# Output projections as seven half-sized products over pairs of 512-token stretches, in place of plain block products

## The chip, the cores and the metric

The kernel runs on one core of one Trainium2 chip. The metric is the device time of one execution in microseconds (us); less is better. The engines are TensorE (PE, with its weight loads shown apart as PEld), VectorE (DVE), ScalarE (ACT), GpSimd (POOL) and SyncE (SP, whose queue issues the transfers). A line number such as L929 is a line of the kernel before.

## The reference, cut to what matters

A decoder layer over 2048 tokens of width 1024 (16 meta tokens are put in front and dropped at the end). One input projection feeds a sliding-window attention branch and an mLSTM branch. What the change touches is the end of it:

```python
y_a = (att * jax.nn.silu(a_z)) @ w_attn_out
y_m = (hm * jax.nn.silu(m_z)) @ w_mlstm_out          # hm: LayerNorm over heads, times head_norm
merged = jax.nn.sigmoid(g_a) * y_a + jax.nn.sigmoid(g_m) * y_m
out = h + rmsnorm(merged @ w_out, norm_post)
```

Each of the three matrices is 1024 x 1024, so there are three products of 2048 x 1024 by 1024 x 1024. Everything is float32.

## The kernel before, in words

**Precision.** A float32 matrix product is made of three matmuls of the type float32r: each operand is split into a rounded part "hi" and a remainder "lo" (`lo = raw - hi`), and hi x hi, hi x lo and lo x hi are added up in one PSUM bank. The rounding is a copy on ACT (L181, L889), the subtraction is DVE's (L182, L890). The operands of the split are plain float32 tiles, 128 partitions by 512 columns (the constant SB).

**The main part** (to about three quarters of the span) goes over two halves of the tokens. For each it runs a plan of 18 column blocks of the input projection (`token_proj`, L703, and `feat_proj`, L715), and weaves the chains of the attention blocks (`attn_block`) and of the mLSTM blocks (`mlstm_chain`) in between: `slot` advances them after every six matmuls. The branches' results go out to memory as att_d and hm_d, feature by token; the gates' as az, mz, ga, gm (`evict_f`). The last two blocks of the plan are those of the gate gm, when all chains of the half are through. PE's order is the order of the program; the other engines' queues are filled by a scheduler by priorities, in which `tc.high_priority(offset=n)` moves instructions ahead by n places. Each engine works its queue in order. In `mlstm_chain` the normalised block, two transposes of 128 columns, is copied out of PSUM by one ACT copy (L611).

**The output projections** (L882 to L971) go over four strips of 512 tokens. For either branch (ph 0 and 1) a strip loads eight tiles of the branch and eight of its gate, multiplies them on DVE (L915; L917 for the mLSTM branch, where the head norm hn_t is a third factor), splits them (`split_unit`, L889 and L890), loads and splits the weights in two halves of eight tiles (`load_w`), and makes eight feature tiles of 24 matmuls each (L929). A bank is evicted on DVE with the merge gate (L934, or L936 and L937), and the merged tile is split at once (L938). Then the third product with w_out (L951) has the merged tiles as the stationary operand; its banks are squared on ACT for the norm (L956), multiplied by gpost (L959, L967), scaled, added to x (L970) and written out. So a strip has 16 + 8 groups of 24 matmuls, 576, and the weights are loaded and split anew in every strip. All tiles of the main part's pools (`units`, `wp`, `stage` and the PSUM pools) stay in use; only the pool `wk` of the main part is closed before, and `p2` takes its place. The operands of the first strip's first branch are loaded ahead by a priority offset of 150.

Of the kernel before, what the change touches and what calls it, by code (L numbers as in the profile page):

```python
# [9 lines left out]
F32 = mybir.dt.float32  # L10
# [80 lines left out]
def hybrid_layer(ctx: ExitStack, tc: tile.TileContext, x, xT, mx, mxT, gpre, w_all, w2, negs, cw, cb,  # L91
# [11 lines left out]
    units = pool("units", 16)  # L103
    wp = pool("wp", 9)
    stage = pool("stage", 4)
    ps_p = pool("ps_p", 2, PSUM)
    ps_s = pool("ps_s", 2, PSUM)
    ps_t = pool("ps_t", 2, PSUM)
    ps_a = pool("ps_a", 2, PSUM)

    def ctile(name, shape, dt=F32):
        return const.tile(shape, dt, name=name)
# [50 lines left out]
    def load_w(src, off, w, p2=None, each=None, lead=SPLIT_LEAD):  # L163
        his, los = [], []
        first = each is not None
        for k in range(KT):
            if first:
                each(k, 0)
            if p2 is None and seq[0] % 5 >= 3:
# [7 lines left out]
            own = p2 is not None and k < 2  # L177
            hi = p2.tile([128, SB], R, name="whi2", bufs=4) if own else wp.tile([128, SB], R, name="whi")
            lo = p2.tile([128, SB], R, name="wlo2", bufs=4) if own else wp.tile([128, SB], R, name="wlo")
# [25 lines left out]
    with ExitStack() as es1:  # L205
# [354 lines left out]
        def mlstm_chain(h, b, j, v1, tho, qT, kT, GT, mrep):  # L560
# [50 lines left out]
            S.copy(tho, th[:, 0:256])  # L611
# [140 lines left out]
        for c in range(NHALF):  # L752
# [7 lines left out]
            for pi, (kind, arg, cols) in enumerate(PLAN):  # L760
# [3 lines left out]
                if c == 0 and pi == 0:  # L764
# [13 lines left out]
                    wh, wl = load_w(w_all, off, w, None, each)  # L778
# [103 lines left out]
    # ---- output projections  # L882
    p2 = pool("p2", 2)
    gpost_t = p2.tile([128, D], F32, name="gpost", bufs=1)
    nc.sync.dma_start(out=gpost_t, in_=gpost.partition_broadcast(128))

    def split_unit(src):
        un = units.tile([128, 2, SB], R, name="un")
        S.copy(un[:, 0], src)  # L889
        tt(un[:, 1], src, f(un)[:, 0], ALU.subtract)  # L890
        return un

    for s in range(SEQ // SB):
        sl = slice(s * SB, (s + 1) * SB)
        part = [None] * KT
        mg = [None] * KT
        for ph, (src, zn, gn) in enumerate(((att_d, "az", "ga"), (hm_d, "mz", "gm"))):
            us = []
            with (tc.high_priority(offset=150) if s == 0 and ph == 0 else ExitStack()):
                for k in range(KT):  # L900
                    early = s == 0 and ph == 0
                    if early:
                        a = p2.tile([128, SB], F32, name=f"part{k}", bufs=1)
                    else:
                        a = stage.tile([128, SB], F32, name="xs")
                    nc.sync.dma_start(out=a, in_=src[k, :, sl])
                    if early:
                        if k % 2 == 0:
                            zz = p2.tile([128, D], F32, name="y", bufs=4)
                        z = zz[:, k % 2 * SB:(k % 2 + 1) * SB]  # L910
                    else:
                        z = p2.tile([128, SB], F32, name="zl", bufs=3)
                    nc.sync.dma_start(out=z, in_=gate_d[zn][k, :, sl])
                    if ph == 0:
                        tt(a, a, z, ALU.mult)  # L915
                    else:
                        stt(a, a, hn_t[:, k:k + 1], z, ALU.mult, ALU.mult)  # L917
                    us.append(split_unit(a))
            for nb_ in range(2):
                wh, wl = load_w(w2, (2 * ph + nb_) * D * SB, SB, p2)  # L920
                for i in range(4):
                    j = nb_ * 4 + i
                    th = p2.tile([128, SB], F32, name="tl", bufs=3)
                    nc.sync.dma_start(out=th, in_=gate_d[gn][j, :, sl])
                    ps = ps_p.tile([128, SB], F32, name="pj")
                    n = 0
                    for k in range(KT):
                        for a, ww in ((0, wh), (1, wh), (0, wl)):
                            T.matmul(ps, lhsT=ww[k][:, 128 * i:128 * i + 128], rhs=us[k][:, a],  # L929
                                     start=(n == 0), stop=(n == 3 * KT - 1))  # L930
                            n += 1
                    if ph == 0:
                        part[j] = p2.tile([128, SB], F32, name=f"part{j}", bufs=1)
                        stt(part[j], th, 1.0, ps, ALU.add, ALU.mult)  # L934
                    else:
                        stt(th, th, 1.0, ps, ALU.add, ALU.mult)  # L936
                        tt(part[j], part[j], th, ALU.add)  # L937
                        mg[j] = split_unit(part[j])  # L938
        w_o = load_w(w2, 4 * D * SB, SB, p2)
        ys, sss = [], []  # L940
        for i in range(4):
            ys.append(p2.tile([128, D], F32, name="y", bufs=4))
            sss.append(p2.tile([128, 4], F32, name="yss", bufs=4))
        for nb_ in range(2):
            wh, wl = w_o if nb_ == 0 else load_w(w2, 5 * D * SB, SB, p2)
            for i in range(4):
                ps = ps_p.tile([128, SB], F32, name="pj")
                n = 0
                for k in range(KT):
                    for a, ww in ((0, wh), (0, wl), (1, wh)):  # L950
                        T.matmul(ps, lhsT=mg[k][:, a, 128 * i:128 * i + 128], rhs=ww[k],  # L951
                                 start=(n == 0), stop=(n == 3 * KT - 1))
                        n += 1
                y, ss = ys[i], sss[i]
                jk = p2.tile([128, SB], BF, name="jk2", bufs=1)
                S.activation(jk, ps, AF.Square, accum_out=ss[:, nb_:nb_ + 1])  # L956
                cs = slice(nb_ * SB, (nb_ + 1) * SB)
                if nb_ == 0:
                    tt(y[:, cs], ps, gpost_t[:, cs], ALU.mult)  # L959
                    ts(ss[:, 2:3], ss[:, 0:1], 1.0 / D, 16.0 * EPS, ALU.mult, ALU.add)  # L960
                    continue
                r0 = s * SB + i * 128
                xr = p2.tile([128, D], F32, name="xr")
                nc.sync.dma_start(out=xr, in_=x[r0:r0 + 128, :])
                ts(ss[:, 2:3], ss[:, 1:2], 1.0 / D, ss[:, 2:3], ALU.mult, ALU.add)  # L965
                G.tensor_tensor(ss[:, 3:4], ss[:, 2:3], mh_t[:, 0:1], ALU.pow)  # L966
                tt(y[:, cs], ps, gpost_t[:, cs], ALU.mult)  # L967
                for j in range(2):
                    cs = slice(j * SB, (j + 1) * SB)
                    stt(y[:, cs], y[:, cs], ss[:, 3:4], xr[:, cs], ALU.mult, ALU.add)  # L970
                    nc.sync.dma_start(out=out[r0:r0 + 128, cs], in_=y[:, cs])  # L971
# [54 lines left out]
```

## Time and profile before

| | |
|---|---|
| three runs | 2420.58, 2423.35, 2424.9 us; median 2423.35 |
| profiled execution: time and span | 2425.5 us |
| granted TensorE clock, mean over the span | 0.994 |
| PE, DVE, ACT, POOL busy, share of the span | 98%, 61%, 42%, 21% |
| output projections: first matmul of L929 to last of L951 | 1875.2 to 2419.5 us |

A share of busy time is an average over parts with different limits; what ends the waits in the part that is changed says more. Matmuls overlap one another, so the record of one (389 ns) is longer than the distance from one to the next. In a timeline a row stands for one or more equal instructions in a row (x2): the first number is when it starts, the second how long it lasts from its first start to its last end. An engine's records overlap a little (a DVE record begins before the one ahead has ended), so the distance of starts tells what one costs in the queue. A record begins when the instruction is taken up, and what it then waits for inside the engine is counted in.

### The profile page before, as it was taken

To read this page: it belongs to the slowest core of one execution; us is meant where nothing else is said; L and a number is where in the kernel's file an instruction comes from. 1 tells how busy PE (TensorE), PEld (TensorE's weight loads), DVE (VectorE), ACT (ScalarE), POOL (GpSimd) and SP (SyncE) were. 2 spreads that over 40 slices of the span, in tenths; PEclk is the share of its full clock that TensorE was granted. 3 is DMA by queue.
4 is the path that set the end of the run, shared out by engine and by line. 5 is a ranking of instruction groups with operands and counts; after the bars stand their busy time and mean duration, and the time that the engine had idled before them with its cause. 6 is when DMAs were issued, how large, how long until landed. Compare 5 with 4: busy or idle time off the path is not lost.

```text
span 2425.5 us, 35347 instructions
## 1 busy us (share of the span) xinstructions
PE 2380.6 (98%) x11725; PEld 2021.0 (83%) x11725; DVE 1469.0 (61%) x4013; ACT 1022.7 (42%) x2674; POOL 517.7 (21%) x1087
## 2 busy tenths in 40 slices
PE   8999999999999999999999999999999999999998
PEld 7788988988888888888988888898888878877787
DVE  7776377367637733677468457637733666665654
ACT  6554354355435423454345345435423333333432
POOL 5332233223233310332323222223310000000000
PEclk8999999999999999999999999999999999999999
DMA  5113212231311234112212212221226768575752
GB/s 188 46 50 101 91 56 67 70 109 42 99 49 58 87 102 142 49 59 70 89 59 58 77 47 65 73 88 56 71 85 226 242 192 263 176 240 168 241 170 92
DMA packets 176167, 261.42 MB, mean 108 GB/s; under 512 B 18684, under 2 KB 68176, under 8 KB 175984
## 3 DMA queue, kind: packets, MB, share of 16 engines
q1 hardware_dynamic: 175984, 259.17, 34.1%
q8 instruction: 92, 1.51, 0.3%
q14 instruction: 91, 0.75, 0.1%
HBM read 200.35 MB, written 58.76 MB: 107 GB/s over the span
## 4 chain that ended last, share of the span: by engine, by line
PE 84%; DMA 6%; DVE 5%; ACT 2%; POOL 1%; issue 1%; SPq 0%; DVEq 0%; POOLq 0%; ACTq 0%
PE pj L715 35%; PE pj L703 22%; PE pj L929 10%; PE pj L951 3%; PE acc L476 3%; PE s L427 3%; DMA wraw<-in_w 3%; DVE wlo L182 2%; PE acc L543 2%; PE tr L449 1%; DMA xs<-att_d 1%; DMA zl<-mz_d 1%; ACT whi L181 1%; PE tr L400 1%; PE tr L543 1%
## 5 line engine op out<-in xcount | busy, mean ns | idle before, releaser
L715 PE MATMUL pj<-un,whi 128*128 128x512 f32 x2560 | 805.0, 396 | 0.0
L703 PE MATMUL pj<-whi,un 128*128 128x512 f32 (+2 forms) x1952 | 604.9, 371 | 0.0
L715 PEld LDWEIGHTS pj<-un,whi 128*128 128x128 f32 x2560 | 467.6, 189 | 88.6
L715 PE MATMUL pj<-un,wlo 128*128 128x512 f32 x1280 | 502.1, 392 | 0.0
L182 DVE TENSOR_TENSOR wlo<-wraw,whi 128x512 fp32r<-128x512 f32 (+2 forms) x480 | 327.1, 704 | 176.1 <-ACT whi L181 173.3
L703 PEld LDWEIGHTS pj<-whi,un 128*128 128x128 f32 x1952 | 361.4, 188 | 38.2 <-issue 1.3
L181 ACT CAST whi<-wraw 128x512 fp32r<-128x512 f32 (+2 forms) x480 | 285.1, 606 | 235.0 <-DMA wraw<-in_w 133.2
L703 PE MATMUL pj<-wlo,un 128*128 128x512 f32 (+2 forms) x976 | 356.3, 365 | 0.0
L929 PE MATMUL pj<-un,whi 128*128 128x512 f32 x1024 | 315.7, 389 | 4.0 <-DVE part L934 4.0
L715 PEld LDWEIGHTS pj<-un,wlo 128*128 128x128 f32 x1280 | 240.7, 188 | 53.1
L929 PEld LDWEIGHTS pj<-un,whi 128*128 128x128 f32 x1024 | 191.9, 188 | 45.4 <-DVE part L934 4.3
L929 PE MATMUL pj<-un,wlo 128*128 128x512 f32 x512 | 199.2, 389 | 0.0
L703 PEld LDWEIGHTS pj<-wlo,un 128*128 128x128 f32 x976 | 184.1, 189 | 15.0
L459 POOL TENSOR_SCALAR_AFFINE_SELECT pp<-pc 128x512 fp32r<-128x512 f32 x120 | 84.0, 700 | 436.0 <-ACT pc L454 420.3
L951 PE MATMUL pj<-whi,un 128*128 128x512 f32 x512 | 163.4, 398 | 10.2 <-DVE y L967 8.1
L728 ACT ACTIVATE xs<-pj 128x512 f32<-128x512 f32 x128 | 76.5, 598 | 213.9 <-PE pj L715 197.8
L433 ACT ACTIVATE P<-s,mn 128x144 f32<-128x144 f32 x256 | 97.5, 381 | 125.5 <-DVE junk L431 122.0
L966 POOL TENSOR_TENSOR yss<-yss,mhalf 128x1 f32<-128x1 f32 x16 | 8.8, 550 | 618.8 <-DVE yss L965 618.8
L951 PEld LDWEIGHTS pj<-whi,un 128*128 128x128 f32 x512 | 98.3, 192 | 33.4 <-DVE y L967 9.3
L929 PEld LDWEIGHTS pj<-un,wlo 128*128 128x128 f32 x512 | 96.1, 188 | 20.0 <-DVE wlo L182 0.2
L951 PE MATMUL pj<-wlo,un 128*128 128x512 f32 x256 | 101.3, 396 | 0.0
L429 DVE COPY_PREDICATED s<-um,s 128x128 f32<-128x128 int32 x240 | 65.7, 292 | 58.5 <-PE s L427 58.1
(334 smaller groups left out, 3373.7 us busy)
## 6 DMA issues: line engine op xcount, KB each, us to landing
wraw<-in_w_all SPq DMA_DIRECT2D x224, 256.0 KB, 3.4
wraw<-in_w SPq DMA_DIRECT2D x192, 256.0 KB, 3.5
wraw<-in_w_all SPq DMA_DIRECT2D x48, 192.0 KB, 2.5
ga_d<-xs SPq DMA_DIRECT2D x32, 256.0 KB, 2.4
att_d<-ao SPq DMA_DIRECT2D x64, 128.0 KB, 1.8
hm_d<-tho SPq DMA_DIRECT2D x64, 128.0 KB, 1.8
az_d<-xs SPq DMA_DIRECT2D x32, 256.0 KB, 2.4
mz_d<-xs SPq DMA_DIRECT2D x32, 256.0 KB, 2.4
```

The costliest lines, as they stand in the source:

```text
L181: S.copy(hi[:, :w], raw[:, :w])
L182: tt(lo[:, :w], raw[:, :w], f(hi)[:, :w], ALU.subtract)
L427: T.matmul(sp[:, c0:272], lhsT=qs[:, h // 2, h % 2, :], rhs=ks[:, i, c0:272], start=(i == 0), stop=(i == 1))
L433: S.activation(P[:, s], sp[:, 128:272], AF.Exp, bias=mn[:, s:s + 1], scale=-1.0, accum_out=mn[:, 4 + s:5 + s])
L459: G.affine_select(pp[:, i], f(pc)[:, i], pattern=[[0, 4], [-1, 128]], compare_op=ALU.is_gt, fill=0.0, base=0, channel_multiplier=1)
L476: T.matmul(acc, lhsT=l, rhs=r.rearrange("p s q -> p (s q)"), start=(i == 0), stop=(i == len(ops) - 1))
L543: T.matmul(out, lhsT=l[:, a], rhs=r[:, b_], start=(start and n == 0), stop=(stop and n == 2))
L703: T.matmul(ps[:, :w], lhsT=us[k][:, a, o:o + 128], rhs=ww[k][:, :w], start=(n == 0), stop=(n == 3 * KT - 1))
L715: T.matmul(ps, lhsT=ww[k][:, 128 * i:128 * i + 128], rhs=us[k][:, a], start=(n == 0), stop=(n == 3 * KT - 1))
L728: S.activation(th, ps, AF.Tanh, scale=0.5)
L929: T.matmul(ps, lhsT=ww[k][:, 128 * i:128 * i + 128], rhs=us[k][:, a], start=(n == 0), stop=(n == 3 * KT - 1))
L951: T.matmul(ps, lhsT=mg[k][:, a, 128 * i:128 * i + 128], rhs=ww[k], start=(n == 0), stop=(n == 3 * KT - 1))
```

## The change

The four strips become two pairs of 512-token stretches, and each of the three products is made for a pair as a 2 x 2 block product in Winograd's form of Strassen's method. The matrix is cut in two along the contraction (512 of 1024) and in two along the output features, the tokens in two along the stretches. Names: w00, w01, w10, w11 are quarters of the weights (first digit the contraction half, second the feature half), b00 to b11 quarters of the data (contraction half, stretch). Seven products of 48 matmuls, P1 to P7, are made of these and of sums and differences of them:

- weights: s3 = w00 - w01, s2 = w11 - s3, s1 = s2 + w00, s4 = w10 - s2, on POOL; s3, s1 and s4 are written over w01, w00 and w10, s2 has two tiles of its own
- data: t1 = b01 - b00, t2 = b11 - t1, t3 = b11 - b01, t4 = b10 - t2, on DVE; t1, t3 and t4 are written in place, t2 has tiles of its own

There are six stages (branch or last product, pair): (0,0), (1,0), (0,1), (1,1), (2,0), (2,1). Tiles are now 128 x 2 x 512, 1024 columns. The gate multiplies az and mz are on POOL, and the head norm is folded into the ACT copy of `mlstm_chain`. The merged tiles go out to memory (mg_d) and are loaded again for the third product, where they are stationary. Each product adds into four PSUM banks; three of seven (P1, P2, P5) begin anew, and the others add to what stands there. P1, P6 and P5 are copied out by ACT to tiles e; the quarters of the result are made on DVE from a bank and e. Loads are issued three products ahead, splits one product ahead. All pools of the main part close before, and the new SBUF pools pB and pA and two PSUM pools of four banks take their place; `rot` spreads the tiles of one kind over pA and pB in turn. The removed lines (L883 to L971 of before) are printed above and stand here as "...":

```diff
@@ pools
-    units = pool("units", 16)
-    wp = pool("wp", 9)
-    stage = pool("stage", 4)
...
+    es1 = ExitStack()
+    mconst = pool("mconst", 1, None, es1)
+    units = pool("units", 16, None, es1)
+    wp = pool("wp", 9, None, es1)
+    stage = pool("stage", 4, None, es1)
...
@@ mlstm_chain
-            S.copy(tho, th[:, 0:256])
+            for i in range(2):
+                S.activation(tho[:, 128 * i:128 * i + 128], th[:, 128 * i:128 * i + 128], AF.Copy,
+                             scale=hn_t[:, 2 * h + i:2 * h + i + 1])
@@ output projections
...
+    PRODS = (("P1", 0, "w00", "b00"), ("P2", 1, "w10", "b10"), ("P6", 0, "s2", "t2"), ("P5", 1, "s1", "t1"),
+             ("P7", 0, "s3", "t3"), ("P3", 1, "s4", "b11"), ("P4", 0, "w11", "t4"))
+    pB = pool("pB", 1)
+    pA = pool("pA", 1)
+    ps_1 = pool("ps_1", 4, PSUM)
+    ps_0 = pool("ps_0", 4, PSUM)
...
+    def rot(kind, shape, dt, in_a, in_b):
+        n = count[kind] = count.get(kind, -1) + 1
+        early = n % (in_a + in_b) < in_a
+        return (pA if early else pB).tile(shape, dt, name=kind + ("A" if early else "B"), bufs=in_a if early else in_b)
+
+    STAGES = ((0, 0), (1, 0), (0, 1), (1, 1), (2, 0), (2, 1))
+    SRC = ((att_d, "az"), (hm_d, "mz"), (mg_d, None))
+
+    def load_b(u, name):
...
+        for p in range(2):
+            k0 = 4 * kh + 2 * p
+            t = rot("rb", [128, 2, SB], F32, 4, 6)
+            nc.sync.dma_start(out=t, in_=src[k0:k0 + 2, :, t0:t0 + SB].rearrange("a p t -> p a t"))
+            if zn is not None:
+                z = pA.tile([128, 2, SB], F32, name="z", bufs=2)
+                nc.sync.dma_start(out=z, in_=gate_d[zn][k0:k0 + 2, :, t0:t0 + SB].rearrange("a p t -> p a t"))
+                G.tensor_tensor(t, t, z, ALU.mult)
...
+    def load_wq(u, name):
...
+        for p in range(2):
+            t = rot("rw", [128, 2, SB], F32, 4, 5)
+            nc.sync.dma_start(out=t, in_=w2[ph, 2 * kh + p, nh])
...
+    LOADS = (("b00", "w00"), ("b10", "w10"), ("b01", "w01", "b11", "w11"), (), (), (), ())
...
+    def combos(u, i):
+        r = raws[u]
+
+        def comb(eng, dst, x_, y_, op, new=None):
+            out_ = []
+            for p in range(2):
+                t = r[new][p] if new else rot("rb" if dst[0] == "t" else "rw", [128, 2, SB], F32,
+                                              4, 6 if dst[0] == "t" else 5)
+                eng.tensor_tensor(t, r[x_][p], r[y_][p], op)
+                out_.append(t)
+            r[dst] = out_
+
+        if i == 2:
+            comb(G, "s3", "w00", "w01", ALU.subtract, "w01")
+            comb(V, "t1", "b01", "b00", ALU.subtract, "b00")
+            comb(G, "s2", "w11", "s3", ALU.subtract)
+            comb(V, "t2", "b11", "t1", ALU.subtract)
+        elif i == 3:
+            comb(G, "s1", "s2", "w00", ALU.add, "w00")
+        elif i == 4:
+            comb(V, "t3", "b11", "b01", ALU.subtract, "b01")
+        elif i == 5:
+            comb(G, "s4", "w10", "s2", ALU.subtract, "w10")
+        elif i == 6:
+            comb(V, "t4", "b10", "t2", ALU.subtract, "b10")
+
+    def prep(n):
+        u, i = divmod(n, len(PRODS))
+        combos(u, i)
...
+        for p in range(2):
...
+            for name, kind, in_a, in_b in ((wn, "ow", 2, 1), (bn, "ob", 2, 2)):
+                src = raws[u][name][p]
+                op = rot(kind, [128, 2, 2, SB], R, in_a, in_b)
+                S.copy(op[:, 0], src)
+                tt(op[:, 1], src, f(op)[:, 0], ALU.subtract)
...
+    def quarter(u, nh, sh, g, bank, e):
+        ph, sc = STAGES[u]
+        if ph == 2:
...
+            if e is None:
+                S.activation(jk, bank, AF.Square, accum_out=ss[:, nh:nh + 1])
+                tt(y, bank, gpost_t[:, cs], ALU.mult)
+            else:
+                tt(y, bank, e, ALU.add)
+                S.activation(jk, y, AF.Square, accum_out=ss[:, nh:nh + 1])
+                G.tensor_tensor(y, y, gpost_t[:, cs], ALU.mult)
+            if not first:
+                finish_rows(sc, sh, g)
+            return
...
+        nc.sync.dma_start(out=th, in_=gate_d["ga" if ph == 0 else "gm"][j, :, t0:t0 + SB])
+        if ph == 0:
+            m = part[nh, sh, g] = pB.tile([128, SB], F32, name="big", bufs=16)
+            if e is not None:
+                tt(m, bank, e, ALU.add)
+            stt(m, th, 1.0, m if e is not None else bank, ALU.add, ALU.mult)
+        else:
+            m = part.pop((nh, sh, g))
+            if e is not None:
+                tt(e, bank, e, ALU.add)
+            stt(th, th, 1.0, e if e is not None else bank, ALU.add, ALU.mult)
+            G.tensor_tensor(m, m, th, ALU.add)
+            nc.sync.dma_start(out=mg_d[j, :, t0:t0 + SB], in_=m)
+
+    with tc.high_priority(offset=300):
+        for n in range(3):
+            loads(n)
+        ops[0] = prep(0)
+    for n in range(N):
...
+        if n + 3 < N:
+            loads(n + 3)
+        if n + 1 < N:
+            with (tc.high_priority(offset=200) if n == 0 else ExitStack()):
+                ops[n + 1] = prep(n + 1)
+        fresh = name in ("P1", "P2", "P5")
...
+        order_ = [(p, g, kk) for p in range(2) for g in range(4) for kk in range(2)]
+        if n == N - 1:
+            order_ = [(p, g, kk) for g in range(4) for p in range(2) for kk in range(2)]
+        for p, g, kk in order_:
+            ow, ob = pairs[p]
+            for m, (a, b) in enumerate(((0, 0), (0, 1), (1, 0))):
...
+                T.matmul(banks[bset][g], lhsT=l, rhs=r, start=(fresh and p == 0 and kk == 0 and m == 0),
+                         stop=(p == 1 and kk == 1 and m == 2), skip_group_check=True)
+        for g in range(4):
...
+            elif name == "P2":
+                quarter(u, 0, 0, g, bk, e1[g])
...
+            elif name == "P7":
+                quarter(u, 1, 1, g, bk, e5[g])
+            elif name == "P3":
+                quarter(u, 0, 1, g, bk, e2[g])
+            else:
+                quarter(u, 1, 0, g, bk, None)
```

`finish_rows` has the last steps of before, for 512 columns at a time: two one-column operations on DVE, the power on POOL, the load of x, and `stt(y[nh], y[nh], ss[:, 3:4], xr, ALU.mult, ALU.add)` on DVE, twice for each of eight row blocks in a stage. The weights w2 are laid out so that one load brings two contraction tiles of one quarter, 512 KB.

## Rows read from the trace of the kernel before

**Rows 1.** The page's head and its busy time by engine.

```profile
span 2425.5 us, 35347 instructions
...
PE 2380.6 (98%) x11725; PEld 2021.0 (83%) x11725; DVE 1469.0 (61%) x4013; ACT 1022.7 (42%) x2674; POOL 517.7 (21%) x1087
```

**Rows 2.** Busy time by stretch, output projections; last columns clock, DMA share, GB/s.

```profile
1875.00:2010.00 135.00, 130.39 (x566) 106.93 (x565) 83.36 (x135) 48.71 (x89) 1.65 (x3) 0.99 0.71 220
...
2285.00:2420.00 135.00, 134.43 (x594) 111.00 (x592) 70.14 (x114) 40.57 (x75) 2.36 (x5) 1.00 0.48 148
sum 545.00, PE 530.21 PEld 434.93 DVE 320.60 ACT 184.82 POOL 8.25; mean PE 132.55 PEld 108.73 DVE 80.15 ACT 46.20 POOL 2.06
```

**Rows 3.** Chain of waits, last strip: start, length, what.

```profile
2288.87 87.04 PE pj L929 x384
2375.91 43.53 PE pj L951 x192
```

**Rows 4.** Source line L929: ns min/median/max, first and last start.

```profile
L929 PE MATMUL pj<-un,whi x1024: 389/389/501, 1875.2 to 2375.3; 128*128 128x512 f32 x171
```

**Rows 5.** Timeline, the last matmul: start, length.

```profile
2419.04 0.39 PE L951 MATMUL pj<-whi,un 128*128 128x512 f32 x1
```

**Rows 6.** Waits in the output projections: us in total, times, longest.

```profile
PE pj L951 <- DVE y L967: 8.1, 3, 3.1
```

**Rows 7.** Timeline of DVE, output projections.

```profile
1960.89 1.89 DVE L182 TENSOR_TENSOR wlo<-wraw,whi 128x512 fp32r<-128x512 f32 x3
```

**Rows 8.** Groups by line and form, whole span: count, busy us, mean ns, idle before.

```profile
L468 POOL TENSOR_TENSOR pmb<-pm,bm 128x512 fp32r<-128x512 f32 x64 | 73.6, 1151 | 0.0
L253 POOL TENSOR_TENSOR qkv<-ropa,ropb 128x96 f32<-128x96 f32 x64 | 29.5, 462 | 5.0
L890 DVE TENSOR_TENSOR un<-xs,un 128x512 fp32r<-128x512 f32 x56 | 36.8, 686 | 3.8 <-ACT un L889 3.4
L182 DVE TENSOR_TENSOR wlo<-wraw,whi 128x384 fp32r<-128x384 f32 x48 | 26.0, 556 | 1.2 <-ACT whi L181 0.8 <-PE pj L715 0.2
L917 DVE SCALAR_TENSOR_TENSOR xs<-xs,hn,zl 128x512 f32<-128x512 f32 x32 | 23.9, 749 | 25.2 <-DMA zl<-mz_d 19.1 <-DMA xs<-hm_d 6.2
L181 ACT CAST whi<-wraw 128x512 fp32r<-128x512 f32 x416 | 252.4, 620 | 223.4 <-DMA wraw<-in_w 133.2 <-PE pj L929 24.9 <-DMA wraw<-in_w_all 24.2
L611 ACT COPY tho<-tr 128x256 f32<-128x256 f32 x64 | 24.0, 375 | 0.0
L578 ACT ACTIVATE kw<-tr,GT 128x128 fp32r<-128x128 f32 x64 | 23.5, 367 | 2.1 <-PE tr L570 2.1
```

**Rows 9.** Timeline of DVE and POOL in the first stage.

```profile
63.94 1.39 DVE L688 SCALAR_TENSOR_TENSOR kT<-kT,gpre,acc 128x512 f32<-128x512 f32 x2
...
64.75 1.30 POOL L694 TENSOR_TENSOR un<-qT,un 128x512 fp32r<-128x512 f32 x1 [1.14 <-ACT un L693]
65.26 0.73 DVE L688 SCALAR_TENSOR_TENSOR pc<-pc,gpre,acc 128x512 f32<-128x512 f32 x1
...
66.52 0.73 DVE L688 SCALAR_TENSOR_TENSOR pc<-pc,gpre,acc 128x512 f32<-128x512 f32 x1
67.18 1.13 DVE L694 TENSOR_TENSOR un<-pc,un 128x512 fp32r<-128x512 f32 x1
...
70.36 1.29 POOL L694 TENSOR_TENSOR un<-pp,un 128x512 fp32r<-128x512 f32 x1 [0.89 <-ACT un L693]
```

**Rows 10.** Timeline of DVE and POOL at the start.

```profile
10.24 3.21 POOL L653 TENSOR_TENSOR xs<-xs 128x512 f32<-128x512 f32 x2
10.63 1.66 DVE L182 TENSOR_TENSOR wlo<-wraw,whi 128x392 fp32r<-128x392 f32 x1
12.22 1.78 DVE L643 SCALAR_TENSOR_TENSOR un<-v,gpre,un 128x512 fp32r<-128x512 f32 x1
13.92 0.55 DVE L182 TENSOR_TENSOR wlo<-wraw,whi 128x392 fp32r<-128x392 f32 x1
```

**Rows 11.** DMA issues: line, count, KB each, us to landing.

```profile
wraw<-in_w SPq DMA_DIRECT2D x192, 256.0 KB, 3.5
```

More of the change, by code (lines that the diff above doesn't have):

```diff
@@ L102, in hybrid_layer @@
     dram = pool("dram", 1, DRAM)
-    units = pool("units", 16)
-    wp = pool("wp", 9)
-    stage = pool("stage", 4)
[L106 to L109, printed above, removed]
+    es1 = ExitStack()
[3 more added lines that the diff above has]
+    stage = pool("stage", 4, None, es1)
+    ps_p = pool("ps_p", 2, PSUM, es1)
+    ps_s = pool("ps_s", 2, PSUM, es1)
+    ps_t = pool("ps_t", 2, PSUM, es1)
+    ps_a = pool("ps_a", 2, PSUM, es1)
     def ctile(name, shape, dt=F32):
-        return const.tile(shape, dt, name=name)
+        return (const if name in ("mhalf", "gpre") else mconst).tile(shape, dt, name=name)
     def f(t):
@@ L161, in hybrid_layer, with load_w @@
     extra = [None]
-    def load_w(src, off, w, p2=None, each=None, lead=SPLIT_LEAD):
+    def load_w(src, off, w, each=None, lead=SPLIT_LEAD):
         his, los = [], []
@@ L168, in load_w @@
                 each(k, 0)
-            if p2 is None and seq[0] % 5 >= 3:
+            if seq[0] % 5 >= 3:
                 raw = extra[0].tile([128, SB], F32, name="wraw2")
@@ L176, in load_w @@
                               in_=src[off + k * 128 * w:off + (k + 1) * 128 * w].rearrange("(p n) -> p n", n=w))
-            own = p2 is not None and k < 2
-            hi = p2.tile([128, SB], R, name="whi2", bufs=4) if own else wp.tile([128, SB], R, name="whi")
-            lo = p2.tile([128, SB], R, name="wlo2", bufs=4) if own else wp.tile([128, SB], R, name="wlo")
+            hi = wp.tile([128, SB], R, name="whi")
+            lo = wp.tile([128, SB], R, name="wlo")
             with (ExitStack() if first else tc.high_priority(offset=lead)):
@@ L777, in each @@
                             u[0][k] = unscaled(0, k)
-                    wh, wl = load_w(w_all, off, w, None, each)
+                    wh, wl = load_w(w_all, off, w, each)
                 else:
@@ L880, in hybrid_layer @@
         drain(True)
-    p2 = pool("p2", 2)
-    gpost_t = p2.tile([128, D], F32, name="gpost", bufs=1)
-    nc.sync.dma_start(out=gpost_t, in_=gpost.partition_broadcast(128))
[L887 to L971, printed above, removed]
@@ new lines, in load_wq, with loads @@
+    def load_wq(u, name):
+        ph = STAGES[u][0]
+        kh, nh = int(name[1]), int(name[2])
+        out_ = []
+        for p in range(2):
+            t = rot("rw", [128, 2, SB], F32, 4, 5)
+            nc.sync.dma_start(out=t, in_=w2[ph, 2 * kh + p, nh])
+            out_.append(t)
+        raws[u][name] = out_
+    LOADS = (("b00", "w00"), ("b10", "w10"), ("b01", "w01", "b11", "w11"), (), (), (), ())
+    def loads(n):
+        u, i = divmod(n, len(PRODS))
+        for name in LOADS[i]:
+            (load_b if name[0] == "b" else load_wq)(u, name)
@@ new lines, in hybrid_layer, with etile, finish_rows @@
+    N = len(STAGES) * len(PRODS)
+    banks = [[None] * 4, [None] * 4]
+    e1, e2, e5 = [None] * 4, [None] * 4, [None] * 4
+    part, ysum = {}, {}
+    def etile():
+        return pB.tile([128, SB], F32, name="e", bufs=8)
+    def finish_rows(sc, sh, i):
+        y, ss = [part.pop((nh, sh, i)) for nh in range(2)], ysum.pop((sh, i))
+        r0 = (2 * sc + sh) * SB + i * 128
+        ts(ss[:, 2:3], ss[:, 0:1], 1.0 / D, 16.0 * EPS, ALU.mult, ALU.add)
+        ts(ss[:, 2:3], ss[:, 1:2], 1.0 / D, ss[:, 2:3], ALU.mult, ALU.add)
+        G.tensor_tensor(ss[:, 3:4], ss[:, 2:3], mh_t[:, 0:1], ALU.pow)
+        for nh in range(2):
+            cs = slice(nh * SB, (nh + 1) * SB)
+            xr = pB.tile([128, SB], F32, name="th", bufs=4)
+            nc.sync.dma_start(out=xr, in_=x[r0:r0 + 128, cs])
+            stt(y[nh], y[nh], ss[:, 3:4], xr, ALU.mult, ALU.add)
+            nc.sync.dma_start(out=out[r0:r0 + 128, cs], in_=y[nh])
```

55 lines of the change are left out of this document (52 added, 3 removed).

## Prediction, made before the change ran

> **What bounds the kernel now.** I read the page's busy shares first, then the last part stage by stage. TensorE (PE) is busy for 98% of the span, VectorE (DVE) 61%, ScalarE (ACT) 42%, GpSimd (POOL) 21% [rows 1]. In four strips of the output projections it is the same picture, with one difference that matters later: POOL does next to nothing there, 8 us in 545, while DVE is at 321 us [rows 2]. The chain of waits ends in two unbroken pieces of matmuls, 384 in 87.04 us and 192 in 43.53 us, so one matmul costs 0.2267 us at a granted clock of 0.99 to 1.00, the upper of the two levels [rows 2, 3]. The output projections run from 1875.2 us to the end of the last matmul at 2419.5 us [rows 4, 5]: **544.3 us**. Their 2304 matmuls (1536 + 768) need 522.3 us of that; the other 22 us are waits, the longest entry of them for a DVE eviction [rows 6]. Behind the last matmul lie 6 us of tail to the end of the span [rows 1, 5]. So the stage is held by PE, and fewer matmuls would shorten it, as long as nothing else becomes longer than PE.
>
> **What is removed on PE.** After the change there are 6 stages of 7 products, each product 2 x 4 x 2 x 3 = 48 matmuls of the same shape: 2016. 288 fewer, times 0.2267, is 65.3 us. PE alone would need 457 us.
>
> **What is added elsewhere.** Count by the code, then price.
>
> DVE, tiles of 1024 columns: 28 splits per stage (two halves, weights and data, 7 products), 168 in all, and 8 differences t1 to t4 per stage, 48. Price: 512 columns follow one another every 0.60 us (three in 1.89 us, the record itself 0.69) [rows 7]; from 384 to 512 columns the record grows from 556 to 686 ns, 1.02 ns a column [rows 8], so 1024 columns take 0.60 + 0.52 = 1.13 us in the queue, and at most twice 0.60. 216 x 1.13 = 244 us. DVE, tiles of 512 columns: in the gate stages 12 adds of bank and e, 4 gates straight from a bank (one input in SBUF) and 12 gates from two SBUF tiles per stage; in the two last stages 16 from a bank and 16 last steps with x. Together 96 with one input in SBUF at 0.60 and 80 with two at 0.66 (the step from 66.52 to 67.18) [rows 9]: 58 and 53 us. With some 4 us of one-column work DVE has **359 us of its own** against the 321 of before.
>
> POOL, 1024 columns: 32 gate multiplies and 48 differences s1 to s4, 80; 512 columns: 32 adds of the branches and 24 multiplies by gpost, 56. None of this was on POOL before. Price: with two plain SBUF inputs 512 columns take 1.29 us (first and last of four at L694) [rows 9], 96 columns 0.46 on average [rows 8]; 0.83 us over 416 columns is 2.0 ns a column, so 1024 columns are 1.29 + 1.02 = 2.3 us. The lower end is L468 (one input repeated), 1.15 us for 512, hence 2.1 or less for 1024; the upper is twice 1.29, 2.6. I take 2.3, and 80 x 2.3 + 56 x 1.29 = 256 us from issue to end. By a size table alone POOL, DVE and PE would all fit into 480 us.
>
> **Why they don't fit side by side.** The rows at the start of the kernel show POOL and DVE working with two SBUF inputs at once. DVE's scalar_tensor_tensor at 12.22 takes 1.78 us and its 392-column subtraction at 10.63 takes 1.66; with POOL idle the subtraction takes 0.55 [rows 10], and L917, the same operation, takes 0.75 everywhere [rows 8]. The excess, 1.0 to 1.1 us each, is the length of one POOL operation, and POOL's own stretch in the same places (two in 3.21 us instead of 2.6). They take turns. At 63.94 and 65.26, beside POOL's L694, DVE reads one input from PSUM (L688's acc) and keeps its 0.73; the next one with two SBUF inputs, at 67.18, takes 1.13 [rows 9]. So what collides is POOL's tensor_tensor with DVE's operations on two SBUF inputs. From the starts at 10.63, 12.22 and 13.92, less DVE's own 0.48 and 0.66, POOL holds DVE off 1.1 and 1.04 us per 512 columns [rows 10]; 0.2 us of its record is not held. For 1024 columns that is 2.3 - 0.2 = 2.1 us. The Trainium skill, page "SBUF — State Buffer", section "Who interferes with whom", has this as an exclusive lock held for the whole instruction, with PSUM-sourced DVE work free of it; by the lock the sum is the one below, without it PE's, and these rows agree with the lock.
>
> **The sum.** Time in which POOL holds: 80 x 2.1 + 56 x 1.05 = 227 us. DVE's own two-input work: 244 + 53 = 297. These exclude one another: **524 us** at least. DVE's other 62 us can lie under POOL's turns, or not: at most 586. POOL is at work or waiting in about half of the time, so I take half hidden: 555 us. Of this some 22 us fall ahead of 1875 us, while the last gate projections run and DVE has idle time: the eight gate multiplies and four splits of the first product, whose operands lie in the early pool (the high priority of 300 is for these). Behind the last split PE still has its 10.9 us product, of which the last evictions cover 6: plus 5. So 538 us as the bound. Then come waits in which DVE has nothing it can do. The clearest one is in the code: a stage asks for ten rw tiles, eight loads and two of s2 (s1, s3 and s4 are written in place), and there are nine. The second half of s2 must take the buffer of w00's first half, which is free only when s1's first half is made and split; that split needs an ow buffer, and there are three. In four of six stages (by the rotation) that buffer is the one that P2 reads to its end. From there: ACT's cast (620 ns for 512 columns [rows 8], so at most 1.24 for 1024), DVE 1.13, POOL 2.3, cast 1.24, DVE 1.13, that is 7.0, and with one turn of the other engine before each of the three about 12 us, against 24 matmuls of P6's first half, 5.4 us. 4 x 6.5 = 26 us. DVE, behind by then, has evictions of P2 to do in this time, so I count all of it as PE's wait and, at worst, as DVE's too: I take 26, ends 0 and 40 (all six stages). 538 + 26 = 564 us against 544.3: **plus 20 us**.
>
> The rest of the edits. The head norm moves from DVE's multiply to the ACT copy of the mLSTM chain, which becomes two of 128 columns: 2 x 0.367 (L578, the same form) for 0.375 [rows 8], 0.36 us x 64 = 23 us of ACT, hidden under PE by ACT's idle 58% [rows 1]; without that cover at most those 23, and I take 0. The weights' 192 loads of 256 KB [rows 11] become 96 of that size in bytes, 24 MB less, while merged rows go out to memory and come back, 16 MB more; DMA was at 0.48 to 0.71 there [rows 2], and SP's queue issues 288 transfers in place of 432: 0, ends -3 and +5. In the queues the in-order cost is POOL's: gate multiplies wait there for transfers, and differences stand behind them. The pools of the main part close before the new ones open; the first product's operands lie in the part that frees early, so I take 0, ends 0 and +7 (two landings of 3.5 us [rows 11] in the open).
>
> The profiled execution took 2425.5 us, its span, and the median of the runs is 2423.35; the difference goes onto the median: 2423 + 20 = **2443 us**.
>
> **Rivals.** (1) *The collisions are cheap.* DVE's PSUM-sourced work lies wholly under POOL's turns and no ring waits: 524 - 17 = 507, against 544.3 that is -37: 2386 us. For: DVE waits of the chain may be filled. Against: DVE and POOL would have to hand the port over without a gap for 500 us, and the small rings keep the queues only one product ahead. With half of it, 2405. Decided by DVE's idle share: below 3%. (2) *PE stays the bound.* 457 + 22 of old waits - 544.3 = -65: 2358 us. The Trainium skill's "Perfetto Trace Analysis", section "Identifying the Most-Contended Engine", would have it so, PE being the busiest. Against it stand rows 10. It holds if two-input operations of 1024 columns do not collide as those of 512 did. (3) *The rings serialize.* Nothing hidden, 586 - 17, and 40 us of waits: 609, +65: 2488 us. For: three ow buffers, ten tiles in nine, and ACT's copies out of PSUM in front of the next casts on its queue. It decides where DVE is idle for more than 7% of the stage.
>
> **How the numbers follow.** Forecast 0.55 (its own range 2425 to 2465), of which 0.05 within 0.2% (about 5 us, what a measurement of this kernel can tell) and 0.50 slower; rival 1 0.20, of which 0.03 within; rival 2 0.07; rival 3 0.18. Faster 0.24, same 0.08, slower 0.68. The range goes from rival 1 to rival 3, 2385 to 2488, and leaves out rival 2 and what lies beyond either end.
>
> **What would show it.** 2016 matmuls at 0.227 us, but PE busy for some 80% of the output stage; POOL from 8 us to some 300 or more there, its 1024-column operations at 2.3 us alone and 3 and more beside DVE; the 1024-column DVE splits at 1.2 us alone and with a mean near 2; DVE busy over 90%; the chain of waits through DVE and POOL instead of two pieces of matmuls; a wait in P6 each stage. If the splits keep 1.2 us beside POOL, the argument is wrong and rival 2 right; if DVE is idle for a fifth, the bound is the rings.

## The result, and the profile after

Before: 2423.62 us, median of 4 runs (2420.58 to 2424.9). After: **2495.03 us**, median of 4 (2491.11 to 2495.58). Ratio 1.0294, interval 1.0279 to 1.0308: slower by 71 us. The forecast was slower by 20, to 2443, the range ended at 2488.

The profiled execution has a span of 2493.0 us, 67.5 more than the one of before. The page's head and busy times:

```profile
span 2493.0 us, 34454 instructions
...
PE 2344.1 (94%) x11437; PEld 1979.5 (79%) x11437; DVE 1660.0 (67%) x3893; ACT 1070.0 (43%) x2690; POOL 864.5 (35%) x1223
```

Beside [rows 1]: 288 matmuls fewer, as counted, POOL up by 347 us, DVE by 191. Busy time by stretch of the kernel after, one row a stage and the tail behind the last matmul; in each row length, then PE, PEld, DVE, ACT and POOL busy, granted clock, DMA share, GB/s:

```profile
1890.00:1994.00 104.00, 84.94 (x335) 67.58 (x336) 93.30 (x59) 36.86 (x43) 69.75 (x23) 0.87 0.64 227
1994.00:2090.00 96.00, 84.25 (x340) 67.09 (x339) 88.97 (x67) 33.95 (x40) 57.95 (x23) 0.93 0.55 184
2090.00:2192.00 102.00, 82.50 (x338) 65.86 (x336) 94.06 (x62) 34.05 (x40) 71.19 (x26) 0.92 0.60 201
2192.00:2288.50 96.50, 83.11 (x337) 66.59 (x336) 86.19 (x68) 33.94 (x40) 52.72 (x22) 0.93 0.51 167
2288.50:2386.00 97.50, 81.85 (x337) 65.76 (x336) 77.50 (x72) 44.39 (x70) 54.16 (x28) 0.93 0.41 136
2386.00:2474.00 88.00, 80.25 (x337) 64.00 (x336) 76.05 (x88) 39.91 (x68) 44.97 (x29) 0.96 0.32 105
2474.00:2493.00 19.00, 0.00 (x0) 0.00 (x0) 8.79 (x14) 0.67 (x2) 1.46 (x3) 0.57 0.82 279
```

Where [rows 2] had PE at 530 us in 545, a stage now takes 88 to 104 us for 336 matmuls that need 76.2 (336 x 0.2267). DVE is busy for 516 us of the six stages' 584, and POOL for 351. The granted clock, 0.99 to 1.00 in [rows 2], is 0.87 to 0.96 here.

The account of the 67.5 us, by the first and last matmuls in the trace:

| part | before | after | difference |
|---|---|---|---|
| start of the output stage (before: first matmul of L929; after: end of the last gate matmul) | 1875.2 | 1873.5 | -1.7 |
| from there to the first matmul of P1 (1890.1) | 0 | 16.6 | +16.6 |
| first to last matmul of the output stage ("body") | 544.3 | 583.8 | +39.5 |
| last matmul to the end of the span ("tail") | 6.0 | 19.1 | +13.1 |

The gap, in the timeline of the kernel after:

```profile
1871.94 0.62 PE L718 MATMUL pj<-un,whi 128*128 128x512 f32 x2
...
1873.07 0.39 PE L718 MATMUL pj<-un,wlo 128*128 128x512 f32 x1
...
1874.17 0.32 SPq L734 DMA_DIRECT2D gm_d<-xs  x1
1876.63 0.37 SPq L916 DMA_DIRECT2D rbA<-att_d  x1
...
1883.19 2.34 POOL L920 TENSOR_TENSOR rbA<-rbA,z 128x1024 f32<-128x1024 f32 x1 [92.14 <-DMA z<-az_d]
...
1890.11 1.22 PE L1069 MATMUL x<-obA,owA 128*128 128x512 f32 x2 [16.64 <-DMA z<-az_d]
```

The stage's first load is issued only behind the last store of a gate tile, and everything runs in the open from there: load, gate multiply, cast, split. The list of SP's waits gives the reason:

```profile
SPq L916 <- DMA gm_d<-xs: 1.8, 1, 1.8
```

A load of rbA has nothing to do with gm_d, except by its place. In the built program's memory map the first buffer of rbA is at bytes 148960 to 153056 of each partition, and the main part's stage pool has two xs buffers between 148672 and 152768. pA begins some 3.8 KB too low.

In the body, PE's waits:

```profile
PE x L1069 <- DVE owA L978: 32.0, 15, 4.8
PE x L1069 <- DVE owB L978: 24.0, 7, 10.4
...
PE x L1069 <- ACT owA L977: 14.6, 2, 7.4
```

and DVE's:

```profile
DVE owA L978 <- ACT owA L977: 40.8, 18, 5.2
DVE owB L978 <- ACT owB L977: 16.6, 8, 3.4
```

Against [rows 6] PE's waits are for operands, not for evictions, and most of DVE's idle time ends at ACT's cast of a weight tile. The groups by line and form tell what is slow (times in us in total, then mean ns):

```profile
L978 DVE TENSOR_TENSOR owA<-rwB,owA 128x1024 fp32r<-128x1024 f32 x31 | 51.8, 1671 | 28.3 <-ACT owA L977 28.3
L978 DVE TENSOR_TENSOR obB<-rbA,obB 128x1024 fp32r<-128x1024 f32 x24 | 50.6, 2110 | 0.1
L920 POOL TENSOR_TENSOR rbA<-rbA,z 128x1024 f32<-128x1024 f32 x16 | 49.5, 3097 | 115.9 <-DMA z<-az_d 95.4 <-DVE owB L978 8.4 <-issue 6.3
L1032 DVE SCALAR_TENSOR_TENSOR big<-th,big 128x512 f32<-128x512 f32 x24 | 33.2, 1411 | 0.0
L1032 DVE SCALAR_TENSOR_TENSOR big<-th,x 128x512 f32<-128x512 f32 x8 | 5.1, 674 | 0.0
L1031 DVE TENSOR_TENSOR big<-x,e 128x512 f32<-128x512 f32 x24 | 15.7, 678 | 0.0
```

Over all 168 splits (L978) the mean is 1.75 us, by groups 1.34 to 2.17. The last three rows are the control within one kernel: L1032 takes 1.41 us with two inputs in SBUF, 0.67 with one of them in PSUM (x), and L1031 likewise keeps 0.68.

The tail, by the end of the chain of waits:

```profile
2473.91 3.85 DMA th<-in_x
2479.07 4.14 DMA th<-in_x
2484.47 4.09 DMA th<-in_x
```

The loads of x come one after another in the open, each waiting for one of four th buffers that DVE frees.

### The profile page after: what moved, and what is told of

Same layout as the page of the kernel before. It is cut to its first block, busy times and chain, and to the rows that moved or that the text cites. A ratio compares the mean times of both kernels' runs of the same rounds, so it can differ in the third digit from the quotient of the medians.

```text
span 2493.0 us, 34454 instructions
## 1 busy us (share of the span) xinstructions
PE 2344.1 (94%) x11437; PEld 1979.5 (79%) x11437; DVE 1660.0 (67%) x3893; ACT 1070.0 (43%) x2690; POOL 864.5 (35%) x1223
## 5 line engine op out<-in xcount | busy, mean ns | idle before, releaser
L718 PE MATMUL pj<-un,whi 128*128 128x512 f32 x2560 | 805.0, 396 | 0.0
L718 PEld LDWEIGHTS pj<-un,whi 128*128 128x128 f32 x2560 | 467.4, 188 | 88.3
L718 PE MATMUL pj<-un,wlo 128*128 128x512 f32 x1280 | 501.6, 392 | 0.0
L706 PEld LDWEIGHTS pj<-whi,un 128*128 128x128 f32 x1952 | 361.5, 188 | 38.3 <-issue 1.3
L718 PEld LDWEIGHTS pj<-un,wlo 128*128 128x128 f32 x1280 | 240.8, 188 | 53.2
L183 DVE TENSOR_TENSOR wlo<-wraw,whi 128x512 fp32r<-128x512 f32 (+2 forms) x288 | 198.4, 714 | 86.4 <-ACT whi L182 84.3
L182 ACT CAST whi<-wraw 128x512 fp32r<-128x512 f32 (+2 forms) x288 | 166.9, 596 | 38.3 <-DMA wraw<-in_w_all 25.0
L1069 PE MATMUL x<-obA,owA 128*128 128x512 f32 x456 | 115.4, 411 | 37.2 <-DMA z<-az_d 16.6
L1069 PE MATMUL x<-obB,owA 128*128 128x512 f32 x456 | 115.6, 412 | 20.7 <-DVE owA L978 15.9
L432 DVE TENSOR_SCALAR_CACHE_REDUCE junk<-s,negs 128x144 bf16<-128x144 f32 x256 | 92.8, 362 | 2.7
```

The costliest lines, as they stand in the source:

```text
L182: S.copy(hi[:, :w], raw[:, :w])
L183: tt(lo[:, :w], raw[:, :w], f(hi)[:, :w], ALU.subtract)
L432: ts(jk, sp[:, 128:272], negs_t[:, 4 * g + h:4 * g + h + 1], None, ALU.min, ALU.min, accum_out=mn[:, s:s + 1])
L706: T.matmul(ps[:, :w], lhsT=us[k][:, a, o:o + 128], rhs=ww[k][:, :w], start=(n == 0), stop=(n == 3 * KT - 1))
L1069: T.matmul(banks[bset][g], lhsT=l, rhs=r, start=(fresh and p == 0 and kk == 0 and m == 0), stop=(p == 1 and kk == 1 and m == 2), skip_grou ...
```

## The experiments

All edits are to the kernel after. "Gap", "body" and "tail" as in the table above. A half of a product is 24 matmuls, which need 24 x 0.2267 us. What the halves of a body take beyond that is called its loss here; for the kernel after it is 127 us, 87 of it in P1 and P6, 22 in P2, 17 in P5. PE is idle for 87 us of the body (584 - 497), so the loss holds some slower matmuls beside the waits.

**e1: POOL's arithmetic on DVE.** In the output stage only the power of one column stays on POOL.

```diff
-                G.tensor_tensor(t, t, z, ALU.mult)
+                V.tensor_tensor(t, t, z, ALU.mult)
...
-            comb(G, "s3", "w00", "w01", ALU.subtract, "w01")
+            comb(V, "s3", "w00", "w01", ALU.subtract, "w01")
```

(and so for s1, s2, s4, the product by gpost and the sum of the branches)

> All of POOL's tensor_tensor work in the output stage (gate multiplies, s1 to s4, gpost, the sum of the branches) is given to DVE; POOL keeps the one-column power. The kernel with the change takes 2495 us, its output stage 584 us from first to last matmul, with 127 us in which PE waits. Theory A (POOL and DVE's two-input operations exclude each other, and DVE is behind because of that): DVE has 359 + 80 x 1.13 + 56 x 0.63 = 485 us of its own and no collisions, so its 1024-column splits fall from means of 1.3 to 2.2 us to 1.2 and the stage to 490 to 520 us: 2400 to 2430 us, faster by 65 us or more although DVE gets 126 us more work. Theory B (the small rings of tiles make PE wait, whoever computes): stage 570 to 590 us, 2480 to 2500. Theory C (POOL's own slowness in the chain s3, s2, s1 of each stage): 6 stages x 4 operations x 1.2 us shorter, some 30 us: 2465.

**e2: POOL only writes.** Each of POOL's tensor_tensor in the stage becomes two memsets of the same tile; that arithmetic is left out.

```diff
+    def twice(t):
+        for _ in range(2):
+            G.memset(t, 0.5)
...
-                G.tensor_tensor(t, t, z, ALU.mult)
+                twice(t)
```

> Each POOL tensor_tensor of the output stage is replaced by two memsets of the same tile, so that POOL stays in the chain for about as long but reads nothing; this leaves out the gate multiplies, the weights' differences s1 to s4, the multiply by gpost and the sum of the branches (constants stand in their place). Theory A with the exclusion on the read side: DVE's splits fall to 1.2 us, the stage to 460 to 500 us, 2370 to 2410. If the exclusion holds for whatever POOL does (its writes too): splits stay at 1.3 to 2.2 us and the time within 25 us of 2495. Theory B: within 15 us of 2495. Theory C: POOL's tiles take 2.1 us for 2.3, so the chain and the time stay within 20 us of 2495.

**e3: pA 4 KB higher.**

```diff
-    gpost_t = pB.tile([128, D], F32, name="gpost")
+    gpost_t = pB.tile([128, 2 * D], F32, name="gpost")[:, 0:D]
```

> The gpost tile is made 4 KB longer, so that the pool pA begins behind the xs tiles of the main part: in the kernel with the change its first tile, rbA, lies over two of the four xs tiles, whose last readers are the stores of the last gate block, and the first load waits for them at 1876.6 us. Theory T (the 17 us between the last gate matmul and the first of P1 come from that overlap): the first loads are issued 30 us or more before the last gate matmul, the gap falls below 3 us, and the time to 2470 to 2480, by 15 to 25 us. Rival (the loads stand behind the gate's stores in SP's queue for another reason, or wait for all of the closed pools): gap and time as before, 2490 to 2500.

**e4: a tenth rw tile.**

```diff
-            t = rot("rw", [128, 2, SB], F32, 4, 5)
+            t = rot("rw", [128, 2, SB], F32, 5, 5)
```

> A tenth rw tile (five in either pool), so that the second half of s2 need not wait until the first half of s1 is split. Theory B: the waits of P6, 43 us of the 127, fall below 15 and the time by 20 to 30 us, 2465 to 2475. Theory A: DVE is behind all the same, the waits move to other products, and the time stays within 8 us of 2495.

These four share a before of 2426.35 us:

| | median | ratio, interval | gap, body, tail |
|---|---|---|---|
| e1 | 2456.66 | 1.0125 (1.0108 to 1.0143) | 16.7, 547.1, 17.3 |
| e2 | 2384.59 | 0.9825 (0.9807 to 0.9844) | 14.9, 475.4, 16.7 |
| e3 | 2479.69 | 1.0223 (1.0205 to 1.0241) | 0, 583.8, 19.6 |
| e4 | 2483.87 | 1.0239 (1.0222 to 1.0256) | 16.6, 571.8, 19.1 |

e2, groups by form:

```profile
L905 POOL MEMSET rwB<- 128x1024 f32 x54 | 51.4, 956 | 85.8 <-DMA rwB<-in_w 43.8 <-DVE owA L985 22.2 <-DVE owB L985 18.5
L985 DVE TENSOR_TENSOR owA<-rwB,owA 128x1024 fp32r<-128x1024 f32 x31 | 37.8, 1221 | 43.6 <-ACT owA L984 43.6
```

and the windows of its body:

```profile
1886.00:2362.00 476.00, 464.30 (x2016) 381.11 (x2016) 353.63 (x412) 225.15 (x301) 212.66 (x283) 0.98 0.64 214
```

POOL is still at work for 213 us, yet the splits take 1.22 us instead of 1.75 (the longest of the 168 takes 1.23), and DVE is busy for 354 us: its own work, priced at 359 in the prediction. The second to fourth stage come out at 76.2 us, PE alone. Splits, body and time are those forecast for an exclusion on the read side. So it is not POOL's being busy that holds DVE; it is POOL's reading. The Trainium skill, page "SBUF — State Buffer", section "Who interferes with whom", says that a DVE instruction with two SBUF inputs contends with a GpSimd instruction that reads SBUF and not with one that only writes it; by that rule, these rows agree.

e1 takes the collisions away and DVE's splits are back at 1.22 us, as theory A has it. Its times, a body of 490 to 520 us and 2400 to 2430 in all, did not come: 90 us of loss stay, 64 of them in one place, the second half of P6. The waits in e1:

```profile
PE x L1069 <- ACT owA L977: 49.3, 6, 16.7
PE x L1069 <- ACT owB L977: 13.6, 2, 10.0
```

That is the second half of s2, the tenth tile in nine buffers; in e5, below, which is e1 with ten, the loss there is 0. With the tenth buffer alone (e4) the loss of P6's second half goes from 23.3 us to 0 and P5's from 17 to 0.4, but the body shortens by 12 only: the first half of P1 loses 13 more, P2 and the first half of P6 8 or 9 each. Neither forecast came, since P6 as a whole still loses 29 (theory B: under 15) and the time is 11 us below 2495 (theory A: within 8). The window of e4's body tells why:

```profile
1892.30:2464.10 571.80, 488.56 (x2016) 393.33 (x2016) 533.70 (x409) 222.90 (x300) 348.55 (x147) 0.92 0.52 176
```

DVE is idle for 38 us, where it was 68 (584 - 516), but busy for 534 instead of 516. Its work is the same, so it is held off for 18 us more: most of the time that the buffer frees goes into collisions.

e3 closes the gap (its first load is issued at 1828.8 us), as theory T has it, and leaves the body at 583.8. Four of the first stage's gate multiplies and four splits now run ahead of the body; DVE is busy in it for 9 us less (507) and idle for 9 more (77). The next four branch loads are issued at 1877.3 us, again only behind the last store of a gate tile.

**e5 to e7: both at once.** e5 is e1 with ten rw buffers, four in pA and six in pB (one more in pB moves pA up, so that no gap is expected), and x loaded in one piece into the z buffers that are free by then. e6 is e5 with POOL's work left on POOL; e7 is e5 with the 32 gate multiplies alone left on POOL.

```diff
-            t = rot("rw", [128, 2, SB], F32, 4, 5)
+            t = rot("rw", [128, 2, SB], F32, 4, 6)
...
-            xr = pB.tile([128, SB], F32, name="th", bufs=4)
-            nc.sync.dma_start(out=xr, in_=x[r0:r0 + 128, cs])
+        xr = pA.tile([128, 2, SB], F32, name="z", bufs=2)
+        nc.sync.dma_start(out=xr, in_=x[r0:r0 + 128, :].rearrange("p (a n) -> p a n", a=2))
```

> Three edits on the kernel with the change: POOL's tensor_tensor work on DVE (as in the first run), a tenth rw tile, which is put into pB so that pA also begins behind the xs tiles, and x for the last rows loaded in one piece into the z tiles, which are free in the last two stages. If collisions, the s2 tile, the overlap of pA and the ring of th tiles are the whole of the loss: the stage from first to last matmul takes 460 to 495 us (PE alone 457, DVE's own 485), the gap ahead of it falls below 3 us and the tail from 19 to under 11, together 2375 to 2395 us, faster than the kernel before by 1.2 to 2%. Rival (DVE with 485 us of uneven work still makes PE wait in P1 to P5): stage over 515 us, 2405 us or more.

> The tenth rw tile in pB and the x loads as in the run above, but POOL keeps its work. If the port is the larger part of the loss: the gap's 15 us, the s2 tile's 11 and some 8 of the tail come off 2495, the rest stays: 2455 to 2468 us, slower than the kernel before by 1.2 to 1.8%. Rival (rings and loads are the larger part): 2435 us or less.

> As the first of these three, but the 32 gate multiplies stay on POOL. If a POOL operation on two SBUF tiles costs DVE the time in which it holds the port (2.1 us where DVE's own operation is 1.13): DVE gets 32 x 0.97 = 31 us worse at most, and the time is 5 to 30 us longer than in that run. Rival (POOL relieves DVE of 36 us): 5 to 30 us shorter, or the same where PE is the bound (within 4 us).

With a before of 2423.34 us:

| | median | ratio, interval | gap, body, tail |
|---|---|---|---|
| e5 | 2385.43 | 0.9851 (0.9836 to 0.9866) | 0, 491.1, 17.7 |
| e6 | 2460.32 | 1.0159 (1.0142 to 1.0175) | 0, 565.9, 19.0 |
| e7 | 2415.21 | 0.9971 (0.9959 to 0.9983) | 0, 520.3, 18.6 |

**e5 beats the kernel before** by 1.5%. The times of all three runs lie in the ranges expected; e5's tail, 17.7 us where under 11 was expected, does not. The windows of the body, e5:

```profile
1877.50:2368.50 491.00, 467.10 (x2017) 379.80 (x2015) 467.33 (x540) 226.87 (x299) 11.89 (x14) 0.99 0.60 200
```

and e6, whose only difference is who does POOL's 136 operations:

```profile
1874.00:2440.00 566.00, 489.00 (x2015) 393.66 (x2013) 522.36 (x406) 223.12 (x301) 349.17 (x146) 0.92 0.52 173
```

The two are 75 us apart. Doing the work itself costs DVE 114 us (467.3 - 353.6, e2's); leaving it to POOL costs DVE 169 (522.4 - 353.6), and 44 us of the body instead of 24 (566 - 522, 491 - 467) in which it has nothing it can start. e7 agrees by the piece: 32 gate multiplies put back make 29.8 us, **0.93 us each**, where DVE takes 1.22 for one. Its groups, one row for each engine:

```profile
L920 POOL TENSOR_TENSOR rbA<-rbA,z 128x1024 f32<-128x1024 f32 x16 | 61.1, 3831 | 218.1 <-DMA rbA<-hm_d 89.0 <-DMA rbA<-att_d 86.0 <-DVE e L1036 29.4
L978 DVE TENSOR_TENSOR obB<-rbA,obB 128x1024 fp32r<-128x1024 f32 x24 | 37.3, 1567 | 0.0
```

POOL's product, 2.34 us alone, takes 3.83 on average in this group and 3.26 over all 32, and the splits of obB 1.57 instead of 1.22: each waits in its turn for the other.

**e8: x ahead; e9: POOL with one input.** e5's tail did not shrink as expected: SP issued a load of x only behind the stores of the row block before. e8 runs those loads three row blocks ahead. e9, on the kernel after, turns each of POOL's operations into a copy of one input; the other input's part is left out.

```diff
+        if len(xs_) < 16:
+            xload(len(xs_))
+        xr = xs_[nfin[0]]
```

```diff
-                G.tensor_tensor(t, t, z, ALU.mult)
+                G.tensor_copy(t, z)
```

> The kernel of e5_dve_rings with one edit: the loads of x run three row blocks ahead, from four buffers (two z tiles and two pairs of th tiles in turn), so that on SP's queue no load of x stands behind the stores of the row block before the one that wants it. Theory (the tail is a ring of buffers and an order on SP's queue): the tail falls from 17.6 us to 8 to 10 (four row blocks at 2 x 0.74 us on DVE, then one store), the body stays at 491 us, the run takes 2375 to 2379 us. Rival (the tail is DVE's work that piles up behind the last matmul, or the stores themselves): the tail stays at 16 us or more and the time at 2384 or more.

> The changed kernel with each tensor_tensor of POOL in the output stage turned into one copy of the same tile with a single input in SBUF (the gate's product, the differences s1 to s4, the product by gpost and the sum of the branches lose one of their inputs; that arithmetic is left out). It tells whether the second input is what collides. Theory A (any read of SBUF by POOL holds DVE's two-input operations off): DVE's 1024-column splits keep a mean near 2 us, the body stays above 550 us, the run takes 2460 us or more. Theory B (only POOL's operations with two inputs in SBUF collide): the splits take 1.22 us as beside the memsets, the body falls to 480 to 500 us, the run takes 2390 to 2415 us.

With a before of 2424.55 us: e8 2383.43 us, ratio 0.9826 (0.9812 to 0.9839), body 495.8, tail 12.0; e9 2391.67 us, ratio 0.9862 (0.9849 to 0.9876), body 482.9, tail 17.1. e8's tail is 5.7 us shorter, its body 4.7 longer, so the whole can't be told from e5's. The longer body is not a longer wait: PE is idle for 24 us of it as in e5, and busy for 472 us instead of 467, at a granted clock of 0.97 instead of 0.99. Of the tail, neither the 8 to 10 of the one reading nor the 16 of the other came out. What is left of the tail is serial: the last two banks' evictions and power follow one another by some 2.2 us, and behind DVE's last operation lie the landings of the last stores:

```profile
2372.38 6.65 SPq L1023 DMA_DIRECT2D out_dram<-big  x8
...
2377.25 1.42 DVE L1022 SCALAR_TENSOR_TENSOR big<-big,yss,th 128x512 f32<-128x512 f32 x2 [0.66 <-POOL yss L1012]
```

e9's groups by form:

```profile
L981 DVE TENSOR_TENSOR owA<-rwB,owA 128x1024 fp32r<-128x1024 f32 x31 | 42.0, 1357 | 33.8 <-ACT owA L980 33.8
L950 POOL COPY rwB<-rwB 128x1024 f32<-128x1024 f32 x15 | 26.7, 1781 | 24.4 <-DVE owB L981 12.2 <-DVE owA L981 8.7 <-DVE yss L998 1.2
```

and the windows of its body:

```profile
1890.00:2373.00 483.00, 467.55 (x2016) 383.23 (x2016) 395.21 (x412) 224.19 (x300) 187.29 (x148) 0.98 0.62 210
```

Theory B's times came, but not its splits: 1.36 us in this group and 1.33 over all 168, not 1.22, and DVE's busy time is 42 us above e2's. So a single read does collide, less: 42 us for 187 of POOL's, against 162 (516 - 354) for 351. How much of the smaller price is the missing input and how much the shorter operation (the quickest copy of 1024 columns took 1.04 us, a product 2.34) these runs don't separate.

## Why the prediction was wrong

**The direction and its reason were right.** PE shrank as counted, and DVE and POOL exclude one another when both read SBUF for two inputs. The prices held: POOL's 1024 columns 2.34 us alone (taken: 2.3) and 3.06 on average over all 80, DVE's own work 354 (359), the split 1.22 alone (1.13 in the queue).

**The collision sum** came out too long. It had 555 us for DVE's own 359 and 196 in which POOL holds it off. Measured in the body are 516: 354 of its own and 162 held off. The 516 lie near the floor of 524, but not for the floor's reason, that DVE's work from PSUM hides under POOL's turns whole. By the records of the kernel after, POOL's operations overlap DVE's from PSUM for 38 of their 61 us; another 37 us of POOL's time lie where DVE is idle and hold nothing off, which the sum did not count.

**The step that failed** is what was put beside that sum, three terms:

- *"Of this some 22 us fall ahead of 1875 us", and 0 for the change of pools.* Nothing fell ahead, since the first load waits for xs, and 17 us of gap took its place. The prediction looked at the order of issue and at which pool closes early, not at the addresses. e3 shows the gap's share by removing it: 15 us by the medians, 17 by the ratios (1.0294 to 1.0223). It also shows that the 22 us are not to be had that way: with the first loads issued some 45 us ahead of the stage, the 9 us that DVE was spared came back as idle time, and the body stayed at 583.8 against the forecast's 564.
- *The waits, 26 us with ends 0 and 40.* DVE is idle for 68 us of the body (584 - 516), 12%, the sign that rival 3 named (over 7%). s2's tenth tile was the right place and about the right size for DVE: e4 takes 30 us of idle time away. But it shortens the body by 12 alone, because the idle time and the held-off time are not independent, and the sum added them as if they were. The other 38 us had no term but the 5 behind the last split: in e4, 26 of them still end at ACT's cast of a weight tile, and 11 at POOL (8 at its one-column power, 3 at a gate multiply). e6, which has the tenth buffer too, has 44 (566 - 522). How this part divides over the small rings, ACT's queue and POOL's order was not tried one by one; its cause stays open.
- *The tail of 6 us, taken as it was.* It is 19. That the last step with x shares four th buffers with its own loads was in the code, and it had no term. e8's edit, on e5, takes back 6 of it.

Together: DVE's own and held-off time 516 for 555, -39 (34 of it in the time held off, 5 in its own work); nothing ahead for 22, +22; idle time 68 for 31 (the 26, and the 5 behind the last split), +37. That is +20 in the body, 583.8 for 564. With the gap's 17, the tail's 13 and the start's -2 outside it: 48 above the forecast of +20, the 67.5 of the two spans.

**The rivals.** Rival 3's time (+65) was nearly right, and its sign, but by luck: its "nothing hidden" was wrong (DVE busy for 516 us, not 586), and the gap and tail, which it did not have, filled the difference. Rival 1's time, 2386, is what e5 reached, but by taking POOL's work away and not by cheap collisions. Rival 2 (PE stays the bound) falls with L978's means; e2, whose POOL is busy for 213 us instead of 351, suggests that it is near what the change would give if POOL didn't read: 2384.59 less the gap of 15 and a tail 10.7 above the old one is 2359, for its 2358.

**ACT, DMA, the head norm** at nothing: ACT is at 223 us of 584 in the body, DMA at 0.51 where it was 0.48 to 0.71, and e2 reaches PE's own pace with both in three stages; the stage starts 1.7 us earlier than before, so the head norm's 23 us of ACT don't show. These hold. Of the signs foretold, DVE over 90% came in only two of six stages (89.0 of 96, 94.1 of 102 us), and the wait in P6 was not alone: P1 lost as much (44 and 43 us).

## What to carry to other kernels

Work moved to GpSimd isn't taken off VectorE when both read SBUF for two inputs: price it by what it keeps VectorE from doing, and compare with VectorE's own time for it; here each product left on GpSimd made the kernel 0.93 us longer than VectorE's doing it itself in 1.22, and all 136 operations 75 us. When TensorE's share is cut by a block scheme, the time that is left is set by operand preparation, so count its tiles against the rings, and look at where new pools lie over old ones: 3.8 KB of overlap opened a gap of 17 us. Look at the end of the kernel too, for a ring that was covered by matmuls before.

## What the runs showed of the hardware that was not expected

GpSimd's memset of 1024 columns took 0.956 us beside VectorE's splits and cost them nothing (1.22 us), while its tensor_tensor work stretched them to 1.75 on average. Its copies, with one input in SBUF, stretched them to 1.33.

TensorE paid for its own waits. After the 17 us gap two matmuls took 1.22 us (at 1890.11), where two took 0.62 ahead of it (at 1871.94), and the granted clock of the stages was 0.87 to 0.96 against 0.99 to 1.00 in [rows 2]: part of the matmuls ran at 1.2 GHz instead of 2.4. The clock went with PE's idle time in the body (the body less PE's busy time): 0.98 and 0.99 in e2 and e5, with 11 and 24 us, 0.96 in e7 with 42, 0.92 in e6 and the kernel after with 76 and 87. The total alone does not fix it, since e8 has 0.97 with 24. Against e2's 464 us of busy PE, the 497 of the kernel after put at most 33 us of its 127 us of loss down to this.
